# Hybrid decoder trunk on one core: the first input also as channel-major blocks, the last residual in halves

## The chip, the cores and the metric

The kernel runs on one core of a Trainium2 chip. The metric is the device time of one execution in microseconds. Before the change three runs took 2188.25, 2188.32 and 2190.48 us; their median is 2188.32 us.

The engines are named as the profile names them: PE does matrix products (PEld is its weight load), DVE is the vector engine, ACT the scalar engine, POOL the general one, SP only issues transfers. A transfer is a DMA.

## The reference, cut to what matters

```python
def rms_norm(x, g):
    y = xf * lax.rsqrt(jnp.mean(xf * xf, axis=-1, keepdims=True) + EPS)
    return y * g
...
for i in range(DEPTH):                      # two layers, 256 tokens, 2048 channels
    if i % 2 == 0:
        h = h + even_mixer(rms_norm(h, even_norm[j]), ...)   # attention | gated delta rule
    else:
        h = h + odd_mixer(rms_norm(h, odd_norm[j]), ...)     # gated position mixing
    h = h + swiglu(rms_norm(h, ffn_norm[i]), ...)
return rms_norm(h, final_norm)
```

Everything is float32. The change touches the first norm, the one ahead of `even_mixer`, and the last one.

## The kernel before

The 256 tokens are two blocks of 128 (`NT`), the 2048 channels four blocks of 512 (`NCH`), each of four blocks of 128 (`KB`). `self.h[t][n]` holds the residual stream, tokens on the partitions, 512 channels in a row.

**Products.** A product needs the channels of its input on the partitions. `fill_unit` transposes a block of `h` on PE (`tok_major`, four transposes into a `side` tile in PSUM), multiplies it by the norm's gain on DVE, and `split` makes a rounded high part on ACT and the remainder on DVE. `dense` does the same to the weights: a DMA brings a block of 512 rows into one of three `raw` buffers, ACT makes `whi`, DVE makes `wlo` (six buffers each), and PE adds three products for each token block: `whi`, `wlo` and `whi` again with the input's remainder. A block of weights is 24 such matmuls, 272 columns wide in the first projection (`kvg`: keys, values and gates of `even_mixer`), 512 wide in the others.

**Norms.** The factor 1/rms is put on after the product. `chunk_stats` squares `h` on ACT and sums along the row (`accum_out`), `end_norm` adds the four sums on DVE and takes the power on POOL; the results `rstd` are used where the sums of a product are read from PSUM.

**Order.** Every instruction is recorded in `Engine.record` (so nearly all have line 178) and `Schedule.plan` (line 189) sets each engine's order: it walks through a model of the engines, takes the ready instruction of the lowest `prio`, and lets none start ahead of its `early` time. Each engine then runs its list strictly in order. SP issues nearly all DMAs, also in order: a block of weights waits on SP until its `raw` buffer is free, and all that stands behind it on SP waits too.

**Start.** `run` (line 1026) loads the identity and the gains, then for each of four channel blocks two blocks of `h`, with the weights of `kvg` between them (`dense(first=True)`, its prio at line 483). PE transposes each block ahead of the products that use it.

**End.** `project` (line 508) writes the last 512 columns (`n = 3`), with PE's products of the second token block kept ten steps behind those of the first (`LAG`). Then `residual` adds the product to `h` on DVE, `chunk_stats` squares on ACT, DVE multiplies `h` by the final gain, and `finish` (line 1014) takes the norm and scales and stores eight blocks.

Of the kernel before, what the change touches and what calls it, by code (L numbers as in the profile page):

```python
# [10 lines left out]
F32R = mybir.dt.float32r  # L11
# [5 lines left out]
P = 128  # L17
D = 2048
# [296 lines left out]
class Trunk:  # L315
# [67 lines left out]

    def load_consts(self):
        nc, t = self.nc, self.t
        self.ident = self.keep((P, P), "ident")
        nc.sync.dma_start(self.ident, t["ident"])
        self.gains = self.const(t["gains"], [P, 4, 16], "gains")
        self.junk = self.keep((P, CW), "junk", BF16)
        self.mhalf = self.keep((P, 8), "mhalf")  # L390
        nc.vector.memset(self.mhalf, -0.5)
        self.phalf = self.keep((P, 8), "phalf")
        nc.vector.memset(self.phalf, 0.5)

    def load_tables(self):
        nc, t = self.nc, self.t
# [54 lines left out]
    def fill_unit(self, srcs, gain=None):  # L451
# [10 lines left out]
            self.split(ps, unit[t])  # L462
        return unit


    def dense(self, w, units, off, width=CW, pcs=None, lag=0, first=False):

        nc = self.nc  # L470
        ps = [self.bank(width) for _ in range(NT)]
        pcs = range(len(units)) if pcs is None else pcs
        size = P * KB * width
        todo = deque()

        def product(t, x, k, hi, lo, st, sp):
            xh, xl = x[t]
            nc.tensor.matmul(ps[t], xh[:, k], hi, start=st, stop=False)
            nc.tensor.matmul(ps[t], xh[:, k], lo, start=False, stop=False)
            nc.tensor.matmul(ps[t], xl[:, k], hi, start=False, stop=sp)  # L480

        for unit, pc in zip(units, pcs):
            with self.prio(2 * pc - 19 if first else 0):
                raw = self.slot((P, KB, width), F32, "raw")
                o = off + pc * size
                nc.sync.dma_start(raw, w[o:o + size].rearrange("(p k n) -> p k n", p=P, k=KB))
            for k in range(KB):
                with self.prio(0):
                    tags = ("unit", "unit") if lag and k % 2 else ("whi", "wlo")
                    hi, lo = [self.slot((P, width), F32R, tag) for tag in tags]  # L490
                    nc.scalar.copy(hi, raw[:, k])
                    nc.vector.tensor_tensor(lo, raw[:, k], hi.bitcast(F32), ALU.subtract)
                with self.prio(9):
                    todo.append((unit, k, hi, lo, pc == pcs[0] and k == 0, pc == pcs[-1] and k == KB - 1))
                    product(0, *todo[-1])
                    if len(todo) > lag:
                        product(1, *todo.popleft())
        with self.prio(9):
            for x in todo:
                product(1, *x)  # L500
        return ps
# [6 lines left out]
    def project(self, w, units, gain, pcs=None):  # L508

        self.begin_norm()  # L510
        size = D * CW if pcs is not None else len(units) * KB * P * CW
        for n in range(NCH):
            self.residual(n, self.dense(w, units, n * size, pcs=pcs, lag=LAG if gain is None and n == NCH - 1 else 0))
            with self.prio(1):
                if gain is not None:
                    self.units.append(self.fill_unit([self.h[t][n] for t in range(NT)], gain[:, KB * n:KB * (n + 1)]))
                self.chunk_stats(n)
                if gain is None:
                    for t in range(NT):
                        self.nc.vector.tensor_tensor(self.h[t][n], self.h[t][n], self.gf[n], ALU.mult)  # L520


    def gate_columns(self, ps):
# [354 lines left out]
    def even_mixer(self, gain):  # L878
        units = self.units
        off, mix, outs, c = 0, [], [], {}  # L880
        for name, cols in EVEN_CHUNKS:
            ps = self.dense(self.t["even_in"], units, off, chunk_width(cols), first=name == "kvg")
            off += D * chunk_width(cols)
            with self.prio(1):
                if name == "kvg":
                    self.end_norm()
                    ba, kk = self.gate_columns(ps), self.attn_kv(ps)
                else:
                    c[name] = self.zgate(ps) if name[0] == "z" else self.tok_tile(ps)
            if name == "kvg":  # L890
                self.schedule.early = 9000.0
                with self.prio(0):
                    self.load_tables()
                self.schedule.early = 0.0
                with self.prio(2):
                    self.gates(ba)
                    kT = self.attn_keys(kk)
            kind, i = name[:-1], int(name[-1]) if name[-1].isdigit() else 0
            with self.prio(2):
                if kind == "k":  # L900
                    keys = self.delta_k(i, c[name])
                elif kind == "q":
                    queries = self.delta_q(i, c[name])
                elif kind == "v":
                    outs.append(self.delta(i, keys, *queries, c[name]))
            with self.prio(3):
                if kind == "qa":
                    mix.append(self.new_unit())
                    for t in range(NT):
                        self.attention(i, t, c[name], mix[i][t], kT)  # L910
        w = self.t["even_out"]
        for n in range(NCH):
            self.residual(n, self.dense(w, mix, n * D * CW, pcs=range(0, 2)))
        with self.prio(1):
            rest = [self.delta_out(outs[i], c[f"z{i}"]) for i in range(2)]
        self.project(w, rest, gain, pcs=range(2, 4))
# [96 lines left out]

    def finish(self):
        nc = self.nc
        self.end_norm()
        for t in range(NT):
            for n in range(NCH):
                o = self.unit(shape=(P, CW))
# [6 lines left out]
    def run(self):  # L1026
        g = lambda i: self.gains[:, i]
        with self.prio(-20):
            self.load_consts()
        self.begin_norm()  # L1030
        self.h = [[None] * NCH for _ in range(NT)]
        for n in range(NCH):
            with self.prio(2 * n - 20):
                self.load_hidden(n)
            with self.prio(1):
                self.units.append(self.fill_unit([self.h[t][n] for t in range(NT)], g(0)[:, KB * n:KB * (n + 1)]))
        with self.prio(1):
            for n in range(NCH):
                self.chunk_stats(n)
        self.even_mixer(g(1))  # L1040
        self.ffn(0, g(2))
        self.odd_mixer(g(3))
        self.ffn(1, None)
        with self.prio(1):
            self.finish()
# [45 lines left out]
def arrays_of(inputs):  # L1091
# [4 lines left out]
    ctab, ident, ltri = const_table()  # L1096
    a = {
        "x": i["x"].reshape(NT, P, NCH, CW).transpose(0, 2, 1, 3),
        "ctab": ctab,
        "ident": ident,  # L1100
        "ltri": ltri,
# [41 lines left out]
```

## Time and profile before

| | |
|---|---|
| median of three runs | 2188.32 us |
| the profiled execution, own time | 2188.75 us |
| its span in the trace | 2186.7 us |
| PE busy, of the span | 2166.3 us (99%) |
| DVE busy | 1326.0 us (61%) |
| ACT busy | 1138.5 us (52%) |
| granted clock of PE, mean | 0.999 |

How to read it: PE is busy nearly all the time, so a change is worth what it takes from PE's queue or from PE's waits, at the place where these lie. The shares of DVE and ACT are means: they are higher in the first 60 us than later. A row of the timeline merges equal instructions that follow each other (x4) and gives the time from the first one's start to the last one's end; durations of neighbours overlap, so the distance between starts says what one costs in a row.

### The profile page before, as it was taken

Reading aid. Unit: us, or ns where it says so; the run is one execution under the profiler, and the core shown is the slowest. Engines: PE = TensorE matmul, PEld = TensorE weight load, DVE = VectorE, ACT = ScalarE, POOL = GpSimd, SP = SyncE. Lnnn points to the kernel's source line nnn. Section 1 sums busy time; section 2 is a strip of 40 time slices with the busy share of each in tenths; the row PEclk is TensorE's granted clock in tenths of the full one; section 3 lists DMA queues with packets and bytes.
Section 4 is the critical chain, followed back from the end, with each engine's and each line's share of the span. In section 5 each row is a group of like instructions: output and inputs, shape, how many; then the busy total and the mean of one; then the engine's idle time right before and its main releaser. Section 6 shows DMA issues by size and latency. Waiting matters only on the chain.

```text
span 2186.7 us, 27199 instructions
## 1 busy us (share of the span) xinstructions
PE 2166.3 (99%) x10044; PEld 1792.4 (82%) x10044; DVE 1326.0 (61%) x2265; ACT 1138.5 (52%) x2034; POOL 59.0 (3%) x68
## 2 busy tenths in 40 slices
PE   8999999999999999999999999999999999999998
PEld 7787888888888888888888888888888888888886
DVE  8796886765555555555555576665555555555553
ACT  7665654554545554444445545554555445444453
POOL 1010100000000000000010000000000000000000
PEclk9999999999999999999999999999999999999999
DMA  7342435555555555555565555555555555565553
GB/s 250 123 156 76 154 117 172 182 186 191 192 193 193 184 187 189 192 193 193 192 237 186 196 168 186 178 189 192 193 185 187 189 192 191 192 209 194 194 195 132
DMA packets 58453, 399.07 MB, mean 183 GB/s; under 512 B 6976, under 2 KB 7232, under 8 KB 11216
## 3 DMA queue, kind: packets, MB, share of 16 engines
q1 hardware_dynamic: 57168, 393.61, 53.0%
q0 software_dynamic: 1152, 3.74, 0.5%
q8 instruction: 78, 1.28, 0.2%
q14 instruction: 55, 0.45, 0.1%
HBM read 395.22 MB, written 2.10 MB: 182 GB/s over the span
## 4 chain that ended last, share of the span: by engine, by line
PE 96%; DVE 2%; ACT 1%; issue 1%; DMA 0%; POOL 0%; SPq 0%; POOLq 0%; DVEq 0%; ACTq 0%
PE mm L178 90%; PE side L178 6%; DVE unit L178 1%; DVE wlo L178 1%; ACT whi L178 0%; DMA h<-in_x 0%; ACT junk L178 0%; POOL unit L178 0%; DVE uc L178 0%; SPq L178 0%; DVE yt L178 0%; DVE h L178 0%; DVE yr L178 0%; ACT L178 0%; ACT unit L178 0%
## 5 line engine op out<-in xcount | busy, mean ns | idle before, releaser
L178 PE MATMUL mm<-whi,unit 128*128 128x512 f32 (+1 forms) x5864 | 1829.8, 391 | 0.0
L178 DVE TENSOR_TENSOR wlo<-raw,whi 128x512 fp32r<-128x512 f32 (+1 forms) x1466 | 1011.0, 691 | 806.0 <-ACT whi L178 800.7
L178 ACT CAST whi<-raw 128x512 fp32r<-128x512 f32 (+1 forms) x1466 | 909.1, 621 | 938.6 <-DVE wlo L178 752.6
L178 PEld LDWEIGHTS mm<-whi,unit 128*128 128x128 f32 x5864 | 1097.8, 188 | 226.0 <-issue 4.7
L178 PE MATMUL mm<-wlo,unit 128*128 128x512 f32 (+1 forms) x2932 | 1140.9, 390 | 0.0
L178 PEld LDWEIGHTS mm<-wlo,unit 128*128 128x128 f32 x2932 | 551.1, 188 | 110.8 <-issue 0.2
L178 PE MATMUL side<-unit,unit 128*128 128x128 f32 (+3 forms) x448 | 60.6, 285 | 0.0
L178 PEld LDWEIGHTS side<-unit,unit 128*128 128x128 f32 (+2 forms) x448 | 54.4, 182 | 5.6 <-issue 1.4
L178 ACT ACTIVATE unit<-mm,rstd 128x512 f32<-128x512 f32 (+1 forms) x84 | 56.1, 671 | 2.2
L178 PE MATMUL side<-ident,unit 128*128 128x128 f32 x356 | 55.0, 273 | 0.4 <-DVE unit L178 0.4
L178 PEld LDWEIGHTS side<-ident,unit 128*128 128x128 f32 x356 | 44.1, 140 | 12.2 <-issue 2.3
L178 DVE TENSOR_TENSOR unit<-side,unit 128x512 fp32r<-128x512 f32 (+1 forms) x64 | 43.6, 690 | 10.8 <-ACT unit L178 10.2
L178 ACT CAST unit<-side 128x512 fp32r<-128x512 f32 x60 | 35.1, 586 | 19.5 <-PE side L178 17.5
L178 DVE TENSOR_TENSOR unit<-unit,unit 128x512 fp32r<-128x512 f32 (+1 forms) x56 | 39.7, 714 | 1.0
L178 PE MATMUL mm<-unit,unit 128*128 128x512 f32 x132 | 35.9, 389 | 0.0
L178 ACT COPY unit<-side 128x512 f32<-128x512 f32 (+1 forms) x36 | 20.6, 585 | 25.4 <-PE side L178 25.4
L178 DVE SCALAR_TENSOR_TENSOR unit<-side,conv,unit 128x255 f32<-128x255 f32 (+2 forms) x72 | 31.1, 473 | 2.4 <-ACT unit L178 2.4
L178 ACT ACTIVATE junk<-h 128x512 bf16<-128x512 f32 x40 | 25.1, 628 | 11.1 <-DVE h L178 8.4
L178 DVE SCALAR_TENSOR_TENSOR unit<-mm,rstd,unit 128x512 f32<-128x512 f32 x44 | 30.9, 743 | 0.0
L178 DVE TENSOR_TENSOR h<-mm,h 128x512 f32<-128x512 f32 x40 | 25.8, 683 | 6.3 <-PE mm L178 6.3
L178 PEld LDWEIGHTS mm<-unit,unit 128*128 128x128 f32 x132 | 24.8, 188 | 5.1
L178 PE MATMUL side<-ident,h 128*128 128x128 f32 x128 | 20.7, 291 | 7.3 <-DMA h<-in_x 7.3
(119 smaller groups left out, 461.4 us busy)
## 6 DMA issues: line engine op xcount, KB each, us to landing
raw<-in_gate SPq DMA_DIRECT2D x88, 1024.0 KB, 4.8
raw<-in_up SPq DMA_DIRECT2D x88, 1024.0 KB, 4.8
raw<-in_down SPq DMA_DIRECT2D x88, 1024.0 KB, 4.9
raw<-in_even_in SPq DMA_DIRECT2D x40, 1024.0 KB, 4.9
raw<-in_odd_in SPq DMA_DIRECT2D x32, 1024.0 KB, 4.9
raw<-in_even_out SPq DMA_DIRECT2D x16, 1024.0 KB, 4.8
raw<-in_odd_out SPq DMA_DIRECT2D x16, 1024.0 KB, 4.9
raw<-in_even_in SPq DMA_DIRECT2D x4, 544.0 KB, 6.7
```

Of the source, the lines that this page charges most:

```text
L178: f(*map(real, args), **{k: real(a) for k, a in kw.items()})
```

## The change

- The host also lays the input out as `xt`: channels on the partitions, 4 x 128 tokens in a row, 256 KB a block as before. `first_unit` loads these eight blocks first, multiplies by the gain and splits; the first four transposes of each of the eight blocks are gone from PE.
- The first norm's sums come from the same blocks: ACT squares each, DVE adds the squares of the four channel blocks (three additions for each token block), and `first_stats` lets PE sum over the partitions, four matmuls against a column of ones for each token block.
- `h` itself is still needed for the residual; its eight DMAs are recorded with `early` 60000.
- The gains are loaded from ACT's queue, the identity later; `kvg`'s weights get another prio; the tables' `early` goes from 9000 to 12000.
- The last 512 columns: `last_chunk` adds the residual in halves of 256, squares each half on ACT as it comes, sums the first three blocks' squares ahead of the end, and multiplies by the final gain into another tile.

```diff
     def load_consts(self):
         nc, t = self.nc, self.t
-        self.ident = self.keep((P, P), "ident")
-        nc.sync.dma_start(self.ident, t["ident"])
-        self.gains = self.const(t["gains"], [P, 4, 16], "gains")
+        self.gains = self.keep((P, 4, 16), "gains")
+        nc.scalar.dma_start(self.gains, t["gains"])
+        with self.prio(-13):
+            self.ident = self.const(t["ident"], [P, P], "ident")
...
+    def first_unit(self, n, gain):
+        unit = []
+        for t in range(NT):
+            x = self.unit()
+            with self.prio(4 * n + 2 * t - 30):
+                self.nc.sync.dma_start(x, self.t["xt"][t, n])
+            with self.prio(4):
+                sq = self.unit()
+                self.nc.scalar.activation(sq, x, AF.Square)
+                if n:
+                    self.nc.vector.tensor_tensor(sq, sq, self.sq[t], ALU.add)
+                self.sq[t] = sq
+            with self.prio(1):
+                y, x = x, self.unit()
+                self.nc.vector.tensor_tensor(x, y, gain.unsqueeze(2).to_broadcast([P, KB, P]), ALU.mult)
+                unit.append([self.unit(F32R), self.unit(F32R)])
+                self.split(x, unit[t])
+        return unit
+
+    def first_stats(self):
+        self.rstd = []
+        with self.prio(4):
+            for t in range(NT):
+                tot = self.side(P, 1)
+                for k in range(KB):
+                    self.nc.tensor.matmul(tot, self.sq[t][:, k], self.ones, start=(k == 0), stop=(k == KB - 1))
+                self.rstd.append(self.rsqrt(tot, [P, 1], 1.0 / D, EPS, "rstd"))
...
-            with self.prio(2 * pc - 19 if first else 0):
+            with self.prio(4 * pc - 29 if first else 0):
...
+            if gain is None and n == NCH - 1:
+                self.last_chunk(n, self.dense(w, units, n * size, pcs=pcs, lag=LAG))
+                break
...
+    def last_chunk(self, n, ps):
+        nc = self.nc
+        half = CW // 2
+        self.rstd = []
+        with self.prio(1):
+            for t in range(NT):
+                a = self.small([P, 1], "a")
+                nc.vector.tensor_reduce(a, self.ss[t][:, :n], AX.X, ALU.add)
+                nc.vector.tensor_scalar(a, a, 1.0 / D, EPS, ALU.mult, ALU.add)
+                h, o = self.h[t][n], self.unit(shape=(P, CW))
+                cs = [slice(i * half, (i + 1) * half) for i in range(2)]
+                sq = self.small([P, 2], "sq")
+                for i, c in enumerate(cs):
+                    nc.vector.tensor_tensor(h[:, c], ps[t][:, c], h[:, c], ALU.add)
+                    nc.scalar.activation(self.junk[:, c], h[:, c], AF.Square, accum_out=sq[:, i:i + 1])
+                nc.vector.tensor_tensor(o, h, self.gf[n], ALU.mult)
+                for i in range(2):
+                    b = self.small([P, 1], "b")
+                    nc.vector.tensor_scalar(b, sq[:, i:i + 1], 1.0 / D, a, ALU.mult, ALU.add)
+                    a = b
+                r = self.small([P, 1], "rstd")
+                nc.gpsimd.tensor_tensor(r, a, self.mhalf[:, 0:1], ALU.pow)
+                self.rstd.append(r)
+                self.h[t][n] = o
...
     def run(self):
...
         for n in range(NCH):
-            with self.prio(2 * n - 20):
-                self.load_hidden(n)
-            with self.prio(1):
-                self.units.append(self.fill_unit([self.h[t][n] for t in range(NT)], g(0)[:, KB * n:KB * (n + 1)]))
+            self.units.append(self.first_unit(n, g(0)[:, KB * n:KB * (n + 1)]))
+        self.first_stats()
+        self.schedule.early = 60000.0
         with self.prio(1):
             for n in range(NCH):
-                self.chunk_stats(n)
+                self.load_hidden(n)
+        self.schedule.early = 0.0
```

What SP has to issue at the start, before. In a row stand the tile, the tensor it comes from and its size; `h` is the token-major input, `raw` the weights of `kvg`:

```order
L178 DMA ident_0_0_4484<-in_ident 128x128
L178 DMA gains_0_1_4486<-in_gains 128x64
L178 DMA h_0_4_4490<-in_x 128x512
L178 DMA h_0_5_4492<-in_x 128x512
L178 DMA raw_76_4494<-in_even_in 128x1088
L178 DMA h_0_20_4496<-in_x 128x512
L178 DMA h_0_21_4498<-in_x 128x512
L178 DMA raw_109_4500<-in_even_in 128x1088
```

And now (`unit` here holds a block of `xt`):

```order
L178 DMA unit_5_4499<-in_xt 128x512
L178 DMA raw_71_4501<-in_even_in 128x1088
L178 DMA unit_10_4505<-in_xt 128x512
L178 DMA unit_15_4509<-in_xt 128x512
L178 DMA raw_104_4511<-in_even_in 128x1088
L178 DMA unit_21_4513<-in_xt 128x512
L178 DMA unit_27_4515<-in_xt 128x512
L178 DMA raw_137_4517<-in_even_in 128x1088
```

The first weights went from the fifth place to the second, behind one block of input instead of two blocks, the identity and the gains; the second token block of the input stands behind them.

DVE's list at the start, before. `side` is the PSUM tile of the transposes, `unit_11` and `unit_18` the high parts that ACT makes:

```order
L178 TENSOR_TENSOR unit_10_4520<-side_6_4512,gains_0_1_4486 128x512
L178 TENSOR_TENSOR unit_17_4529<-side_13_4522,gains_0_1_4486 128x512
L178 TENSOR_TENSOR unit_12_4535<-unit_10_4520,unit_11_4531 128x512
L178 TENSOR_TENSOR unit_19_4539<-unit_17_4529,unit_18_4533 128x512
L178 TENSOR_TENSOR wlo_78_4550<-raw_76_4494,whi_77_4537 128x272
L178 TENSOR_TENSOR wlo_86_4557<-raw_76_4494,whi_85_4543 128x272
```

And now (`unit_5`, `unit_10` and `unit_15` are blocks of `xt`):

```order
L178 TENSOR_TENSOR unit_7_4527<-unit_5_4499,gains_0_0_4495 128x512
L178 TENSOR_TENSOR unit_9_4533<-unit_7_4527,unit_8_4531 128x512
L178 TENSOR_TENSOR unit_12_4539<-unit_10_4505,gains_0_0_4495 128x512
L178 TENSOR_TENSOR wlo_73_4543<-raw_71_4501,whi_72_4535 128x272
L178 TENSOR_TENSOR wlo_81_4549<-raw_71_4501,whi_80_4537 128x272
```

The first remainder of the weights (`wlo_73`) stands behind the multiplication of `unit_10`, the third transfer of SP's list. Further down, the additions of the squares (six of 128x512) stand between the remainders of the second projection's weights, and two rows `side<-ones,unit 128x1 x4` stand on PE among that projection's matmuls.

DVE's list at the very end, for the second token block, before; `mm` is the product, `unit_12905` the final gain:

```order
L178 TENSOR_TENSOR h_0_53_4510<-mm_14071_22892,h_0_53_4510 128x512
L178 TENSOR_TENSOR h_0_53_4510<-h_0_53_4510,unit_12905_21275 128x512
L178 TENSOR_REDUCE tot_0_14385_23276<-ss_0_13272_21890 128x1
L178 TENSOR_SCALAR rstda_0_14386_23278<-tot_0_14385_23276 128x1
L178 TENSOR_SCALAR unit_14396_23284<-h_0_5_4492,rstd_0_14387_23280 128x512
```

And now:

```order
L178 TENSOR_TENSOR h_0_70_5315<-mm_14060_22907,h_0_70_5315 128x256 x2
L178 TENSOR_TENSOR unit_14381_23296<-h_0_70_5315,unit_12894_21284 128x512
L178 TENSOR_SCALAR b_0_14382_23299<-sq_0_14378_23294,a_0_14375_22885 128x1
L178 TENSOR_SCALAR b_0_14383_23301<-sq_0_14378_23294,b_0_14382_23299 128x1
L178 TENSOR_SCALAR unit_14393_23307<-h_0_64_5298,rstd_0_14384_23303 128x512
```

The sum over the four blocks is gone from the end, the residual comes in two pieces, and the product with the gain no longer overwrites what ACT squares.

## Rows read from the trace of the kernel before

**Rows 1.** The chain of work that ended last, by engine, from the page.

```profile
PE 96%; DVE 2%; ACT 1%; issue 1%; DMA 0%; POOL 0%; SPq 0%; POOLq 0%; DVEq 0%; ACTq 0%
```

**Rows 2.** Busy time by stretch of the span: us, then busy time and instructions of PE, PEld, DVE, ACT and POOL, granted clock of PE, busy share of the DMA engines, GB/s.

```profile
4.00:10.00 6.00, 2.68 (x12) 2.31 (x13) 3.59 (x7) 4.05 (x11) 0.00 (x0) 1.00 0.99 340
24.00:50.00 26.00, 24.75 (x123) 20.45 (x122) 23.30 (x65) 17.99 (x44) 7.98 (x6) 1.00 0.56 190
120.00:180.00 60.00, 58.88 (x328) 50.04 (x327) 51.20 (x153) 35.04 (x81) 6.23 (x8) 1.00 0.41 141
240.00:300.00 60.00, 58.79 (x294) 48.54 (x293) 57.19 (x166) 37.75 (x86) 11.15 (x12) 1.00 0.46 156
600.00:2100.00 1500.00, 1500.00 (x6741) 1242.74 (x6740) 856.70 (x1276) 754.29 (x1233) 15.30 (x22) 1.00 0.56 191
```

**Rows 3.** Timeline of PE at the start: start us, us from the first start to the last end, operation, in brackets the idle time before it and what ended that.

```profile
4.58 1.94 PE L178 MATMUL side<-ident,h 128*128 128x128 f32 x8 [4.58 <-DMA h<-in_x]
9.27 1.97 PE L178 MATMUL side<-ident,h 128*128 128x128 f32 x8 [2.74 <-DMA h<-in_x]
10.88 0.80 PE L178 MATMUL mm<-whi,unit 128*128 128x272 f32 x2
11.48 0.43 PE L178 MATMUL mm<-wlo,unit 128*128 128x272 f32 x1
11.71 0.43 PE L178 MATMUL mm<-whi,unit 128*128 128x272 f32 x1
...
13.44 0.60 PE L178 MATMUL side<-ident,h 128*128 128x128 f32 x4
13.79 0.37 PE L178 MATMUL mm<-whi,unit 128*128 128x272 f32 x1
...
18.47 0.41 PE L178 MATMUL mm<-whi,unit 128*128 128x272 f32 x2
18.72 0.29 PE L178 MATMUL mm<-wlo,unit 128*128 128x272 f32 x1
...
25.91 0.75 PE L178 MATMUL mm<-whi,unit 128*128 128x272 f32 x3
26.50 0.39 PE L178 MATMUL mm<-wlo,unit 128*128 128x512 f32 x1
```

**Rows 4.** The queue of SP at the start, from its timeline.

```profile
0.74 0.39 SPq L178 DMA_DIRECT2D ident<-in_ident  x1
1.66 0.90 SPq L178 DMA_DIRECT2D h<-in_x  x2
2.60 0.43 SPq L178 DMA_DIRECT2D raw<-in_even_in  x1
```

**Rows 5.** DVE and ACT at the start, from their timelines.

```profile
4.47 0.63 ACT L178 ACTIVATE junk<-h 128x512 bf16<-128x512 f32 x1 [2.45 <-DMA h<-in_x]
8.63 1.38 ACT L178 CAST whi<-raw 128x272 fp32r<-128x272 f32 x4 [0.72 <-DMA raw<-in_even_in]
...
5.71 0.69 DVE L178 TENSOR_TENSOR unit<-side,gains 128x512 f32<-128x512 f32 x1 [4.80 <-PE side L178]
17.02 0.78 DVE L178 TENSOR_TENSOR wlo<-raw,whi 128x272 fp32r<-128x272 f32 x2
17.72 1.29 DVE L178 TENSOR_TENSOR unit<-unit,unit 128x512 fp32r<-128x512 f32 x2
23.57 0.69 DVE L178 TENSOR_TENSOR unit<-unit,unit 128x512 fp32r<-128x512 f32 x1
```

**Rows 6.** PE between 34 and 40 us, and DVE beside it, from the timeline.

```profile
34.28 0.96 PE L178 MATMUL side<-gg,unit 128*128 128x16 f32 x8
35.09 0.49 PE L178 MATMUL mm<-wlo,unit 128*128 128x512 f32 x1
...
37.37 1.54 DVE L178 TENSOR_TENSOR wlo<-raw,whi 128x512 fp32r<-128x512 f32 x1
...
40.04 0.70 PE L178 MATMUL side<-unit,one 128*128 128x512 f32 x2 [1.25 <-DVE unit L178]
```

**Rows 7.** The end, from the timeline: the last product, then what stands between it and the stores.

```profile
2176.93 0.84 PE L178 MATMUL mm<-unit,unit 128*128 128x512 f32 x3
2177.81 0.69 DVE L178 TENSOR_TENSOR h<-mm,h 128x512 f32<-128x512 f32 x1 [3.09 <-PE mm L178]
2178.59 0.63 ACT L178 ACTIVATE junk<-h 128x512 bf16<-128x512 f32 x1 [4.43 <-DVE h L178]
2179.13 0.19 ACT L178 ACTIVATION_READ_ACCUMULATOR junk<-h 128x1 f32 x1
2179.35 0.69 DVE L178 TENSOR_TENSOR h<-h,unit 128x512 f32<-128x512 f32 x1 [0.85 <-ACT junk L178]
2179.96 0.15 DVE L178 TENSOR_REDUCE tot<-ss 128x1 f32<-128x4 f32 x1
2180.14 0.15 DVE L178 TENSOR_SCALAR rstda<-tot 128x1 f32<-128x1 f32 x1
2180.37 0.55 POOL L178 TENSOR_TENSOR rstd<-rstda,mhalf 128x1 f32<-128x1 f32 x1 [6.97 <-DVE rstda L178]
```

**Rows 8.** DMA issues: KB each, median us from issue to landing; and what SP's queue waited for (us in total, times, longest).

```profile
raw<-in_even_in SPq DMA_DIRECT2D x40, 1024.0 KB, 4.9
...
SPq L178 <- DVE wlo L178: 1885.6, 355, 15.6
```

More of the change, by code (lines that the diff above doesn't have):

```diff
@@ L393, in load_consts @@
         nc.vector.memset(self.phalf, 0.5)
+        self.ones = self.keep((P, 1), "ones")
+        nc.vector.memset(self.ones, 1.0)
     def load_tables(self):
@@ L512, in project @@
         for n in range(NCH):
-            self.residual(n, self.dense(w, units, n * size, pcs=pcs, lag=LAG if gain is None and n == NCH - 1 else 0))
+            if gain is None and n == NCH - 1:
+                self.last_chunk(n, self.dense(w, units, n * size, pcs=pcs, lag=LAG))
+                break
+            self.residual(n, self.dense(w, units, n * size, pcs=pcs))
             with self.prio(1):
@@ L885, in even_mixer @@
                 if name == "kvg":
-                    self.end_norm()
                     ba, kk = self.gate_columns(ps), self.attn_kv(ps)
@@ L890, in even_mixer @@
             if name == "kvg":
-                self.schedule.early = 9000.0
+                self.schedule.early = 12000.0
                 with self.prio(0):
@@ L1015, in finish @@
         nc = self.nc
-        self.end_norm()
         for t in range(NT):
@@ L1029, in run @@
             self.load_consts()
-        self.begin_norm()
+        self.units, self.sq = [], [None] * NT
         self.h = [[None] * NCH for _ in range(NT)]
         for n in range(NCH):
-            with self.prio(2 * n - 20):
-                self.load_hidden(n)
-            with self.prio(1):
-                self.units.append(self.fill_unit([self.h[t][n] for t in range(NT)], g(0)[:, KB * n:KB * (n + 1)]))
+            self.units.append(self.first_unit(n, g(0)[:, KB * n:KB * (n + 1)]))
+        self.first_stats()
+        self.schedule.early = 60000.0
         with self.prio(1):
             for n in range(NCH):
-                self.chunk_stats(n)
+                self.load_hidden(n)
+        self.schedule.early = 0.0
         self.even_mixer(g(1))
@@ L1098, in arrays_of @@
         "x": i["x"].reshape(NT, P, NCH, CW).transpose(0, 2, 1, 3),
+        "xt": i["x"].reshape(NT, P, NCH, KB, P).transpose(0, 2, 4, 3, 1),
         "ctab": ctab,
```

## The prediction

> **What bounds the kernel now.** I read the chain of waits first: 96% of it lies on PE [rows 1]. The table by stretch says where PE is not already saturated: between 600 and 2100 us it is busy 1500.00 of 1500 us, so nothing that this change does elsewhere can help or hurt there unless it adds work to PE [rows 2]. What is left is the start, the waits of the first layer's mixer (1.1 us between 120 and 180 us, 1.2 us between 240 and 300 us, and one of 1.25 us at 38.8 us [rows 2, 6]), and the end after the last product.
>
> The start: PE waits 4.58 us for the first block of `h`, transposes, and waits 2.74 us for the next block [rows 3]. From 9.27 us on it hardly pauses; the first `kvg` matmuls show at 10.88 us, the last one starts at 25.91 us; the two behind it in that row are 512 wide and belong to the next projection [rows 3]. Beside it DVE makes all remainders, and its last one for `kvg` starts at 23.57 us [rows 5]: DVE and PE end this stage within 2 us of each other (24.26 and 26.04 us), so taking work from PE alone is not enough. At the end, 2.56 us lie between the start of the last residual (2177.81) and that of POOL's power (2180.37) [rows 7], and the stores behind it don't change.
>
> The sum is made against the profiled execution: its span is 2186.7 us, its own time 2188.75 us, and that is 0.43 us above the median of 2188.32.
>
> **The start.** I compare one point of the program: all 96 `kvg` matmuls and the next projection's first four done, since PE's new order puts those four ahead of `kvg`'s last ten. Before, `kvg` ends at about 25.91 + 0.13 = 26.04 us; four 512-wide matmuls at 0.225 us each (three take 0.84 us, one 0.39 us, so 0.45 us for two more [rows 7]) make it 26.94 us.
>
> Now the blocks of the input come in the layout that the products need, so DVE begins with the block itself: no transposes, no wait for PE. What DVE waits for is the input. Its third instruction multiplies the second token block, which is SP's third transfer, and all remainders of the weights stand behind that. When does it land? The first of the bulk transfers is issued at 0.74 us now, where the identity was, not at 1.66 us [rows 4]. Ahead of the block's end lie 256 + 32 + 544 + 256 KB = 1.11 MB; at the 340 GB/s of this stretch [rows 2] that is 3.3 us. On top comes a lag between issue and flow. Before, the first block of `h` landed at 4.47 us [rows 5], 2.8 us after its issue, of which 0.8 us are its own bytes: lag 2.0 us. The first weights landed at 8.63 us [rows 5] with 1.08 MB, 3.2 us, from the same issue: lag 3.8 us. So the block lands between 0.74 + 3.3 + 2.0 = 6.0 and 7.8 us. I take 7.0 us: the row of the first weights is the nearer one in bytes, but there the identity and the gains stood ahead, some 0.9 us of issue.
>
> From 7.0 us DVE has in its list, until the last remainder for `kvg`: 14 multiplications and remainders of the input at 0.60 us (two take 1.29 us, one 0.69 us), 8.4 us; 16 remainders of the weights at 0.35 us (two take 0.78 us, one 0.43 us), 5.5 us; two 512-wide remainders of the next projection, 1.2 us [rows 5]. That is 15.1 us, and I add 0.5 us for moments in which it waits for ACT's rounded part, so 22.6 us. Ten matmuls of 0.125 us (two starts 0.25 us apart for a pair, at 18.47 and 18.72 us [rows 3]) stand behind it: 23.9 us. PE alone would be done earlier: from about 8 us, 96 x 0.125 = 12 us, 1.8 us for a slow beginning as before (matmuls 0.23 us apart between 11.48 and 11.71 us [rows 3]) and 0.9 us, so 22.7 us; DVE decides. Gain: 26.94 - 23.9 = **3.0 us**; with the block at 7.8 us it is 2.2 us, with 6.0 us at most 4.0 us, since the second weights then decide. The 16 transposes that PE did at full pace (0.35 to 0.44 us for four, 13.44 to 13.79 us and the longer distance behind [rows 3]) and eight of the slow ones are contained in this.
>
> The rule on PE's clock in the Trainium skill (page "TensorE: Matmul & The Clock Gate", section on the HAM clock gate) speaks against thinning out PE's start: the clock is halved until the array has been kept busy, and gaps keep it halved. The granted clock reads 1.00 between 4 and 10 us, the level of 2.4 GHz [rows 2], yet matmuls lie 0.23 us apart at 11.5 us and 0.125 us at 18.5 us [rows 3], after eight transposes that were followed by a gap, so the distances agree with the rule and the column doesn't show it. By the rule the whole of `kvg` at the lower level is a rival, below; by the rows alone the slow part is the 1.8 us above.
>
> **The sums of the first norm.** Four matmuls against a column of ones, twice. The nearest row is `side<-gg,unit`, four matmuls of the program that the trace shows as eight: from 34.28 us to the next start at 35.09 us, 0.81 us [rows 6]. Twice that is **1.6 us** on PE, now bound there; if PE happens to wait for DVE, it costs 0. I take 1.6 us, because the remainders are ahead at that place. ACT's squares were there before. DVE gets six additions of 0.60 us = 3.6 us, spread between remainders. Between 24 and 50 us DVE idles 26 - 23.3 = 2.7 us [rows 2], and it reaches that stretch some 1.7 us earlier: 4.4 us of cover, so I cost it at 0; without cover it is up to 3.6 us. The sums come later by some remainders, so `kvg` is read from PSUM later; the bank is needed only after the whole next projection, 96 x 0.225 = 21.6 us, hidden. POOL's two powers and the gates behind them move along with it, and the wait of 1.25 us at 38.8 us, where DVE's remainder took 1.54 us beside POOL [rows 6], moves too: 0, with 1.25 us either way.
>
> **The later loads of `h`.** Eight issues of 0.47 us [rows 4] now stand on SP between two blocks of weights, about 60 us in. Blocks wait on SP anyway for DVE to free the buffer (1885.6 us in 355 waits [rows 8]). PE eats one block of 24 matmuls in 5.4 us, so 3.8 us of issues fit into one wait. Of 2.1 + 1.05 MB at 340 GB/s, 9.3 us, 3.9 us are left when the next block is issued; it lands 3.9 + 4.9 us [rows 8] later, 8.8 us, and is due two blocks later, at 10.8 us. Hidden, 2 us to spare. The gains on ACT's queue stand ahead of a table load with nothing behind them: 0.
>
> **The end.** First half of the residual 0.43 us (as a 272-wide remainder [rows 5]), 0.09 us to ACT, two half squares with their sums. A 512-wide square takes 0.54 us and its sum 0.19 us [rows 7]; four 272-wide casts take 1.38 us [rows 5], 0.33 us for one behind another, so a half is 0.52 us: 1.04 us. The product with the gain runs beside this. Then one small instruction of 0.15 us and 0.23 us from its start to POOL's [rows 7], which contains it, and 0.03 us ahead: 1.82 us against 2.56 us. **0.7 us** gained, between 0.3 and 0.9 us.
>
> **Sum.** 3.0 - 1.6 + 0.7 = 2.1 us. 2188.75 - 2.1 = 2186.65 us for the profiled execution, and with the 0.43 us to the median 2186.2 us. A measurement of this kernel tells some 0.2% (4.4 us) from no change, so I expect a gain that is hardly to be told.
>
> **The rivals.**
> - The lead is lost in the mixer. DVE is busy 57.19 of 60 us between 240 and 300 us and 23.30 of 26 us between 24 and 50 us [rows 2]; where PE waits for it, arriving earlier only lengthens the wait. For it: the waits of 1.1 and 1.2 us there. Against it: they are small beside the stretches, and PE does other products meanwhile. Only the end's 0.7 us stays: 2187.6 us.
> - All falls well: the block lands at 6.0 us (4.0 us), the eight small matmuls fall into waits (0), the 1.25 us wait goes: 4.0 + 0.7 + 1.25 = 5.9 us, 2182.4 us.
> - Slower, DVE: the six additions delay the remainders of the second projection. With no cover, 3.6 us of additions and 1.6 us of small matmuls stand against 3.0 + 0.7 us: 2189.8 us. It decides from the point where DVE's idle time between 24 and 50 us falls below 1.5 us.
> - Slower, PE's clock: all 96 matmuls 0.227 us apart. From 8 us that ends at 29.8 us, 30.7 us with the next four, 3.8 us after the old point, and 1.6 - 0.7 us more: 2193.0 us. Against it: at that pace PE would have no gaps, and in rows 3 unbroken work from 9.27 us brought the short distances before 13.44 us.
> - It doesn't do what it says, the late loads of `h` not hidden: they cost up to 9.3 us less the 2 us to spare, less the 2.1 us gained: 2193.5 us.
>
> **How the numbers follow.** Forecast 0.56, lead lost 0.20, all well 0.10, DVE 0.09, clock 0.03, late loads 0.02. The forecast's own bounds are: start 2.2 to 4.0, small matmuls 0 to 1.6, the wait at 38.8 us 1.25 either way, the end 0.3 to 0.9 us; together rarely beyond 2183.4 us below. Above, the range takes in the lost lead whole and most of the DVE case: to 2189.2 us. Faster by over 0.2% (below 2183.9 us): most of "all well" and a little of the forecast, 0.11. Slower by over 0.2% (above 2192.7 us): clock and late loads, 0.05. The rest, 0.84, is within.
>
> **What would show it.** In the changed profile: DVE's first multiplication ahead of 4 us, its third instruction at about 7 us, the last remainder for `kvg` ending at about 22.6 us, PE's last 272-wide matmul at about 23.9 us. Rows `side<-ones` of about 0.8 us for each group. No longer waits of PE for `wlo` between 24 and 60 us than before; raw blocks still landing in time around 60 us. At the end, 1.8 us between the first half residual and POOL's power. It is wrong if DVE's third instruction starts past 8 us, if matmuls stay 0.23 us apart past 15 us, if PE waits for remainders among the additions of squares, or if the waits between 60 and 345 us grow by what the start gained.

## The result and the profile after

The changed kernel takes 2197.35 us, median of six runs (2194.71 to 2199.18), beside 2188.86 us (2188.25 to 2190.48) for the kernel before: ratio 1.0039, 95% interval 1.0028 to 1.0049. It is 8.5 us slower, where a gain of 2.1 us was forecast (2186.2 us, with bounds of 2183.4 and 2189.2 us). The profiled execution has a span of 2195.5 us, against 2186.7 us.

First the table by stretch, with the columns of [rows 2]; the five stretches of [rows 2] are in it, and four more from 60 to 75 us.

```profile
4.00:10.00 6.00, 3.23 (x12) 2.92 (x13) 5.03 (x11) 5.33 (x12) 0.00 (x0) 1.00 1.01 387
24.00:50.00 26.00, 25.12 (x126) 20.68 (x125) 21.74 (x52) 15.57 (x35) 5.56 (x6) 1.00 0.56 198
...
60.00:63.00 3.00, 0.00 (x0) 0.00 (x0) 1.47 (x6) 1.31 (x5) 0.00 (x0) 1.00 1.00 378
...
64.00:65.00 1.00, 1.00 (x10) 0.78 (x6) 1.00 (x3) 0.00 (x0) 0.00 (x0) 0.64 1.05 402
65.00:74.00 9.00, 9.00 (x25) 6.87 (x25) 5.04 (x13) 2.91 (x10) 0.00 (x0) 0.50 0.07 26
74.00:75.00 1.00, 1.00 (x5) 0.82 (x4) 0.64 (x2) 1.00 (x5) 0.00 (x0) 0.74 0.07 16
...
120.00:180.00 60.00, 57.02 (x320) 47.60 (x318) 50.20 (x154) 35.79 (x83) 9.17 (x10) 1.00 0.38 126
240.00:300.00 60.00, 58.77 (x292) 48.78 (x291) 56.66 (x160) 37.45 (x81) 11.16 (x12) 1.00 0.44 144
600.00:2100.00 1500.00, 1500.00 (x6741) 1243.12 (x6740) 857.14 (x1276) 755.56 (x1235) 14.90 (x22) 1.00 0.57 191
```

The granted clock is the share of the full clock that PE was given. PE is idle from 60 to 63 us. It then has work without a break, and about a microsecond into that work its clock halves: granted 0.64, then 0.50 (the level of 1.2 GHz) for nine microseconds, then 0.74. In clock alone that is 0.36 + 4.5 + 0.26 = 5.1 us lost. A second loss lies between 120 and 180 us, 3.0 us idle against 1.1 us [rows 2]. In the other stretches of the table PE's idle time is as before or less.

Next the timeline of the start, PE then DVE, which answers to [rows 3, 5].

```profile
6.01 0.60 PE L178 MATMUL mm<-whi,unit 128*128 128x272 f32 x1 [6.01 <-ACT whi L178]
7.37 0.60 PE L178 MATMUL mm<-wlo,unit 128*128 128x272 f32 x1 [0.77 <-DVE wlo L178]
...
24.31 0.29 PE L178 MATMUL mm<-whi,unit 128*128 128x272 f32 x1
24.44 0.40 PE L178 MATMUL mm<-wlo,unit 128*128 128x512 f32 x1
...
28.08 0.94 PE L178 MATMUL side<-ones,unit 128*128 128x1 f32 x8
28.89 0.72 PE L178 MATMUL mm<-whi,unit 128*128 128x512 f32 x2
...
32.21 0.95 PE L178 MATMUL side<-ones,unit 128*128 128x1 f32 x8
33.02 0.49 PE L178 MATMUL mm<-wlo,unit 128*128 128x512 f32 x1
...
4.29 0.69 DVE L178 TENSOR_TENSOR unit<-unit,gains 128x512 f32<-128x512 f32 x1 [3.36 <-DMA gains<-in_gains]
...
6.28 0.69 DVE L178 TENSOR_TENSOR unit<-unit,gains 128x512 f32<-128x512 f32 x1
...
22.09 0.69 DVE L178 TENSOR_TENSOR unit<-unit,unit 128x512 fp32r<-128x512 f32 x1
```

The last `kvg` matmul gives way to the next instruction at 24.44 us. At that point the same 96 and four matmuls are done for which the prediction worked out 26.94 us before, so the start is 2.50 us shorter. Each group against the ones stands 0.81 us ahead of the next start. Now where the statistics (the sums and powers of the first norm) lead to: POOL's powers, the gates' matmuls, and what I call the decay chain, the instructions that turn the gates into the decay factors of the gated delta rule. At its end DVE and ACT read one `side` tile.

```profile
33.00 1.07 POOL L178 TENSOR_TENSOR rstd<-rstda,mhalf 128x1 f32<-128x1 f32 x2 [32.55 <-DVE rstda L178]
...
41.60 0.96 PE L178 MATMUL side<-gg,unit 128*128 128x16 f32 x8
...
46.31 0.73 PE L178 MATMUL side<-unit,one 128*128 128x512 f32 x2 [0.88 <-DVE unit L178]
...
57.73 2.26 PE L178 MATMUL side<-unit,unit 64*128 64x128 f32 x24
...
59.97 0.28 DVE L178 SCALAR_TENSOR_TENSOR unit<-side,tb,unit 128x64 f32<-128x64 f32 x1 [0.38 <-ACT unit L178]
...
60.28 0.31 ACT L178 ACTIVATE unit<-side,tail 128x64 f32<-128x64 f32 x1 [0.35 <-DVE unit L178]
...
60.63 0.28 DVE L178 SCALAR_TENSOR_TENSOR unit<-side,gam,unit 128x64 f32<-128x64 f32 x1 [0.38 <-ACT unit L178]
...
62.63 0.28 DVE L178 SCALAR_TENSOR_TENSOR unit<-side,tb,unit 128x64 f32<-128x64 f32 x1 [0.38 <-ACT unit L178]
...
63.06 1.99 PE L178 MATMUL side<-unit,unit 64*128 64x128 f32 x16 [3.07 <-DVE unit L178]
64.98 0.79 PE L178 MATMUL mm<-wlo,unit 128*128 128x512 f32 x1
```

The same places in the timeline of the kernel before:

```profile
23.50 3.43 POOL L178 TENSOR_TENSOR rstd<-rstda,mhalf 128x1 f32<-128x1 f32 x2 [23.05 <-DVE rstda L178]
...
53.87 0.27 DVE L178 SCALAR_TENSOR_TENSOR unit<-side,tb,unit 128x64 f32<-128x64 f32 x1
...
54.80 0.71 ACT L178 ACTIVATE unit<-side,tail 128x64 f32<-128x64 f32 x3
...
57.76 4.60 PE L178 MATMUL side<-unit,unit 64*128 64x128 f32 x48
```

The powers are done some 7 us later (34.07 against 26.93 us). The gates' matmuls stand at 41.60 us against 34.28 us [rows 6]. The first attention's score matmuls begin at the same time in both, 57.7 us. Before, DVE's last read of the last decay tile had ended at 54.1 us and ACT's at 55.5 us, and the score matmuls ran through. Now the last read ends at 62.9 us, 7.4 us later. On the way DVE waits 0.38 us for ACT and ACT waits 0.35 us for DVE, with a read of DVE every 0.67 us. There are four `side` tiles, three groups of scores fill three by 59.99 us (57.73 + 2.26), and the fourth belongs to the chain until its last read; 0.15 us after that PE goes on.

The second loss is one wait for POOL:

```profile
122.87 0.50 PE L178 MATMUL side<-unit,same 128*128 128x512 f32 x1 [2.19 <-POOL unit L178]
```

Last the end, which answers to [rows 7]. From the first half residual to POOL's power it is 2.01 us, where it was 2.56 us.

```profile
2187.23 0.76 DVE L178 TENSOR_TENSOR h<-mm,h 128x256 f32<-128x256 f32 x2 [3.59 <-PE mm L178]
2187.75 0.42 ACT L178 ACTIVATE junk<-h 128x256 bf16<-128x256 f32 x1 [4.66 <-DVE h L178]
...
2188.94 0.21 DVE L178 TENSOR_SCALAR b<-sq,b 128x1 f32<-128x1 f32 x1
2189.24 0.55 POOL L178 TENSOR_TENSOR rstd<-b,mhalf 128x1 f32<-128x1 f32 x1 [6.91 <-DVE b L178]
```

### The profile page after: what moved, and what is told of

The parts are those of the page before. It is cut to its first block, busy times and chain, and to the rows that moved or that the text cites. A ratio compares the mean times of both kernels' runs of the same rounds, so it can differ in the third digit from the quotient of the medians.

```text
span 2195.5 us, 27173 instructions
## 1 busy us (share of the span) xinstructions
PE 2171.2 (99%) x10028; PEld 1794.0 (82%) x10028; DVE 1329.6 (61%) x2276; ACT 1139.0 (52%) x2030; POOL 57.5 (3%) x68
## 4 chain that ended last, share of the span: by engine, by line
PE 95%; DVE 3%; ACT 1%; issue 1%; POOL 0%; DMA 0%; POOLq 0%; DVEq 0%; ACTq 0%
PE mm L178 89%; PE side L178 6%; DVE unit L178 1%; DVE wlo L178 1%; ACT whi L178 0%; POOL unit L178 0%; ACT unit L178 0%; DMA gains<-in_gains 0%; DVE uc L178 0%; ACT junk L178 0%; DVE yt L178 0%; DVE yr L178 0%; ACT L178 0%; POOLq L1199 0%; DVE ucp L178 0%
## 5 line engine op out<-in xcount | busy, mean ns | idle before, releaser
L178 DVE SCALAR_TENSOR_TENSOR unit<-side,conv,unit 128x254 f32<-128x254 f32 (+2 forms) x72 | 30.5, 474 | 3.9 <-ACT unit L178 3.7
L178 DVE TENSOR_TENSOR h<-mm,h 128x512 f32<-128x512 f32 (+1 forms) x42 | 26.0, 658 | 6.8 <-PE mm L178 6.8
L178 ACT ACTIVATE junk<-h 128x512 bf16<-128x512 f32 (+1 forms) x34 | 20.5, 602 | 8.5 <-DVE h L178 8.4
L178 ACT CAST unit<-unit 128x512 fp32r<-128x512 f32 x32 | 19.8, 618 | 9.6 <-DVE unit L178 9.4
```

The costliest lines, as they stand in the source:

```text
L178: f(*map(real, args), **{k: real(a) for k, a in kw.items()})
```

## The experiments

Theory A: late statistics push the decay chain into the first attention; PE waits 3.1 us, and its clock then halves. Rival B: the eight late loads of `h`, which run from 56 to 65 us with the DMA engines full, do it. Rival C: it is the wait of 2.2 us for POOL near 122 us, and the other order of instructions up to 165 us. The first three kernels set these against each other. Each ratio below is to the kernel before, timed beside that run.

**Statistics early again (e1)**, in `first_unit` and `first_stats`:

```
-            with self.prio(4):
+            with self.prio(1):
```

> The changed kernel with one number altered: the first norm's squares, additions and ones matmuls get priority 1 in the planner in place of 4, so that the statistics, and with them the gates and the decay chain, come as early as they did before the change. Theory A (late statistics push the decay chain into the first attention's score matmuls, TensorE idles 3.1 us and its granted clock then falls to 0.5 for some 10 us): both are gone, what is left is the start's 2.5 us less the 1.6 us of the ones matmuls and the 0.55 us of the end, 2188.9 - 1.5 = 2187.4 us, 2185.5 to 2189.0. Rival B (the eight late loads of h saturate the DMA engines at 56 to 65 us and hold the weights up): they are as late as in the changed kernel, so the stall stays, about 2197 us. Rival C (the waits of 2.2 us on GpSimd near 122 us and the other order up to 165 us cost most of it): most of the 8.5 us stays, above 2192 us.

Measured: 2188.54 us, ratio 1.0002 (0.9992 to 1.0011). The loss of 8.5 us is gone, and so are the wait at 60 us and the wait for POOL. That speaks against B, but doesn't settle it: the loads of `h` kept their `early` time, and yet SP issues them at 64.15 us here, against 56.45 us in the changed kernel. 2188.5 us is a microsecond above A's 2187.4 us, inside A's range. The squares and additions now stand among the casts and remainders at the start, and PE waits there for DVE and ACT. Its timeline, in the profile of the one run of ten that took 2193.7 us (the other nine lie between 2188.2 and 2189.7 us):

```profile
8.49 0.59 PE L178 MATMUL mm<-wlo,unit 128*128 128x272 f32 x1 [2.39 <-DVE wlo L178]
...
15.93 0.39 PE L178 MATMUL mm<-whi,unit 128*128 128x272 f32 x1 [1.37 <-ACT unit L178]
...
20.59 1.70 PE L178 MATMUL side<-ones,unit 128*128 128x1 f32 x8
...
44.27 0.73 PE L178 MATMUL side<-unit,one 128*128 128x512 f32 x2 [1.82 <-DVE unit L178]
```

What sets this run apart is a granted clock of 0.50 in two places, from 19 to 25 us behind the wait of 1.37 us (and one of 0.69 us at 17.13 us), and from 46 to 49 us behind the wait of 1.82 us. So in this profile early statistics cost PE waits at the start, where the changed kernel has 0.77 and 0.64 us of them. That the microsecond in the medians comes from these waits isn't shown; the interval is wider than a microsecond.

**Loads of `h` later (e2)**, in `run`:

```
-        self.schedule.early = 60000.0
+        self.schedule.early = 150000.0
```

> The changed kernel with the eight loads of h given to the queue 13 blocks of weights later (planner time 150 us in place of 60 us); the order on TensorE, VectorE, ScalarE and GpSimd is untouched, word for word. Theory A: the stall at 60 us and the half clock behind it stay, 2197.4 us, 2195.5 to 2199. Rival B: without the loads at 56 to 65 us the stall is gone, about 2187.4 us. Rival C: 2197.

Measured: 2197.77 us (2193.73 to 2198.16), ratio 1.0034 (1.0020 to 1.0048), as A said. The wait of 3.07 us is there again (at 62.65 us). The DMA engines have nothing to do behind it, and PE is at half its clock all the same; in a row stand PE's busy time and instructions, the granted clock, the DMA share and GB/s:

```profile
65.00:70.00 5.00, 5.00 (x17) 0.50 0.00 0
```

B is out.

**The kernel before with late sums (e3)**, in `even_mixer`:

```
+                    self.schedule.early = 28000.0
                     self.end_norm()
+                    self.schedule.early = 0.0
```

> The kernel before the change with one alteration: the two reductions and powers of the first norm may not be planned before 28 us of the planner's time, so that the gates come some 5 to 8 us later than they did, as in the changed kernel; loads, squares, transposes of the start and the end stay as before. Theory A: the decay chain now meets the first attention, TensorE waits 2 to 4 us near 60 us and its granted clock falls, 2188.9 + 3 to 9 = 2192 to 2198 us. Rivals B and C (late loads of h, or the changed start): neither is in this kernel, 2188.9 us, 2188 to 2190.

Measured: 2191.04 us, ratio 1.0011 (1.0002 to 1.0021); nine runs at 2190.0 to 2192.2 us and one at 2195.7 us, with a mean granted clock of 0.996 where the nine have 0.999. Late sums alone, with the old start, loads and end, cost 2.2 us. That is under A's 3 to 9 us and above what B and C allow (2188 to 2190 us). The powers come as late as in the changed kernel (they end at 33.63 us), and the timeline of the first run (2192.24 us) shows the collision, smaller:

```profile
57.28 2.26 PE L178 MATMUL side<-unit,unit 64*128 64x128 f32 x24
60.66 1.71 PE L178 MATMUL side<-unit,unit 64*128 64x128 f32 x16 [1.12 <-ACT unit L178]
```

Here the two engines read the tile in longer pieces, DVE seven times in a row 0.19 us apart. That suggests that the lateness needs a second thing to make PE wait 3 us, the turns; e5 tests it. The wait accounts for 1.12 of the 2.2 us; where the rest lies isn't shown.

**The end alone (e4)**, `last_chunk` and `finish` of the changed kernel in the kernel before (the diff is the change's own).

> The kernel before the change with the last chunk alone done by halves. By the traces the last matmul to the last power is 0.55 us shorter in the changed kernel, so 2188.9 - 0.55 = 2188.3 us under every theory of the middle; a rival in which the shorter end is lost to the last stores gives 2188.9.

Measured: 2188.14 us, ratio 0.9995 (0.9986 to 1.0004). The 0.7 us agree with the trace, and the interval doesn't tell them from nothing.

**DVE's reads of the last decay tile in one piece (e5)**, after the plan:

```
+        h = self.tiles[self.whole]
+        reads = [op for op in order if op.engine == "dve" and h in op.tiles]
+        i = order.index(reads[0])
+        rest = [op for op in order if op not in reads]
+        order = rest[:i] + reads + rest[i:]
...
+            if gr == 1 and t == 1:
+                self.schedule.whole = rep.tensor.name
```

(`rep` is the decay tile; the one marked is the last of the four.)

> The changed kernel; the order on TensorE, ScalarE, GpSimd and the queues is untouched, and on VectorE the eight reads of the last decay tile in PSUM stand in one piece, ahead of one weight remainder, where that remainder had stood behind the first of them; the eight reads of the same tile by ScalarE then stand behind all of VectorE's, where they had stood between them in turn. Theory A, refined: the two engines' reads of one PSUM tile wait for each other in the written order, which in the changed kernel makes eight steps of 0.67 us (57.84 to 62.9 us) and holds the tile that the fourth group of score matmuls needs until 63.06; in one piece the eight take 1.6 us on VectorE and about 1 us more on ScalarE, the tile is free near 60.5 us, the wait falls from 3.07 to 0.3 to 1.0 us and the half clock behind it goes: 2197.4 - 2.4 - 5.1 = 2189.9 us, 2188.5 to 2192. If the clock falls for another reason than the wait: 2195. If the wait is the sum of the engines' work and not their turns: 2197.

Measured: 2191.16 us, ratio 1.0018 (1.0008 to 1.0027). Seven of ten runs lie at 2190.6 to 2192.2 us (mean granted clock 0.998 to 0.999), three at 2194.9 to 2195.8 us (0.996 to 0.997). Timelines of DVE, ACT and PE in the profile of one of the three:

```profile
58.92 0.28 DVE L183 SCALAR_TENSOR_TENSOR unit<-side,gam,unit 128x64 f32<-128x64 f32 x1
59.12 0.27 DVE L183 SCALAR_TENSOR_TENSOR unit<-side,tb,unit 128x64 f32<-128x64 f32 x1
...
60.15 1.33 ACT L183 ACTIVATE unit<-side,tail 128x64 f32<-128x64 f32 x6
...
61.54 1.71 PE L183 MATMUL side<-unit,unit 64*128 64x128 f32 x16 [1.62 <-ACT unit L183]
```

and two stretches of its table, with the columns as for e2, the second with the wait ahead of it:

```profile
65.00:70.00 5.00, 5.00 (x16) 0.50 0.09 31
...
119.82 0.50 PE L183 MATMUL side<-unit,same 128*128 128x512 f32 x1 [2.19 <-POOL unit L183]
121.00:125.00 4.00, 4.00 (x13) 0.57 0.46 195
```

One remainder on DVE changed its place, and nothing else. DVE's reads come 0.19 us apart, not 0.67, and PE's wait falls from 3.07 to 1.62 us (expected 0.3 to 1.0). ACT needs 2.1 us behind DVE's last read, where about 1 us had been expected: six of its reads take 1.33 us, and one more and a 512-wide instruction stand ahead of them. The turns were 1.45 us of the wait. The lower mean clock comes in three runs of ten, not in all. In the profiled one of the three, PE drops to half its clock twice, behind the wait of 1.62 us and behind the wait of 2.19 us for POOL; which of the two it was in the other runs isn't shown. The seven other runs have a median of 2190.97 us.

**The first attention behind the chain (e6)**, in `even_mixer`, the statistics as late as before:

```
+                    self.schedule.early = 62000.0
                     for t in range(NT):
                         self.attention(i, t, c[name], mix[i][t], kT)
+                    self.schedule.early = 0.0
```

> The changed kernel with the first attention not planned before 62 us of the planner's time, so that its score matmuls stand behind the decay chain and projection matmuls fill TensorE meanwhile; the statistics stay as late as in the changed kernel. Theory A: no wait near 60 us, the granted clock stays at 1.00, 2189.5 us, 2187.5 to 2191. If late statistics cost by themselves, through the gates or the projections that need the powers: the loss stays, above 2194.

Measured: 2186.80 us, ratio 0.9993 (0.9983 to 1.0002). The whole loss is gone, and the time lies below A's 2189.5 us and its range: the wait for POOL near 122 us, which A's figure had kept, is gone as well. The powers come as late as in the changed kernel (33.31 us against 33.00 us), so late statistics don't cost by themselves.

**The kernel before, made to wait (e7, e8)**, in the first attention:

```
+            if kv == 0 and t == 0 and r == 0:
+                self.schedule.unseen = True
+                for i in range(8):
+                    nc.vector.tensor_tensor(s[:, :, 0], qT, qT, ALU.add)
+                self.schedule.unseen = False
```

(While `unseen` is set, the planner counts an instruction at 0 us; e8 has `range(4)`.)

> The kernel before the change with eight additions of 0.60 us (128x512, results overwritten) ahead of the first attention's first mask addition on VectorE, counted at nothing by the planner, so that every other instruction stands where it stood. By the rows of before the first mask addition moves from 59.2 to 64.0 us, and TensorE, which has three groups of scores and one free PSUM tile ahead of it, waits about 3 us. Theory A (a wait of 3 us at this place is followed by some 10 us at half clock): 2188.8 + 3 + 5 = 2196.8 us, 2194 to 2198, granted clock 0.50 behind the wait. If the clock of the changed kernel fell for another reason (its start, its loads, its other order): 2188.8 + 3 = 2191.8 us and a granted clock of 1.00.

> The same with four additions: the first mask addition moves by 2.4 us, and TensorE waits about 0.6 us. Theory A: a short wait leaves the clock at 1.00, 2188.8 + 0.6 = 2189.4 us, 2188.5 to 2190.5. If any wait here makes the clock fall: 2194.

Measured with eight additions: 2195.27 us, ratio 1.0033 (1.0019 to 1.0046), mean granted clock 0.997 in all five runs (0.998 to 0.999 in the 26 of the kernel before). With four: 2189.38 us, ratio 1.0004 (0.9995 to 1.0014), 0.998 to 0.999 in all ten, behind a wait of 0.36 us. PE's timeline with eight:

```profile
57.06 3.16 PE L179 MATMUL side<-unit,unit 64*128 64x128 f32 x32
63.36 3.21 PE L179 MATMUL side<-unit,unit 64*128 64x128 f32 x16 [3.14 <-DVE unit L179]
66.50 0.79 PE L179 MATMUL mm<-whi,unit 128*128 128x512 f32 x1
```

and one stretch of its table, with the columns as for e2:

```profile
65.00:70.00 5.00, 5.00 (x16) 0.50 0.01 3
```

Nothing of the change is in this kernel: old start, old loads, old statistics, old order. A wait of 3.14 us is followed by half the clock. POOL's first power of the next norm comes 6.2 us later (451.14 against 444.99 us), although this profile was 0.7 us ahead at the first powers (22.81 against 23.50 us), so the two cost about 6.8 us; the medians say 7.0 us. This shows the second half of A by itself.

**The better kernel once more, and its control (e9, e10).** The control is the same delay of the first attention in the kernel before.

> The kernel of e6_attention_later again, word for word, timed in more rounds, since its interval touched no change: with the wait and the half clock gone, what the change gains at its start (2.5 us) and end (0.55 us) less the ones matmuls (1.62 us) should be left, 1.4 us below the kernel before, about 2187 us, ratio 0.9993 (0.9988 to 0.9998). If the gain of 1.5 us was chance: ratio 1.000.

> The kernel before the change with the same delay of the first attention as in e6_attention_later and nothing else: in the kernel before, the first attention met no wait, so by theory A the delay brings nothing, 2188.5 us, ratio 1.000 (0.9995 to 1.0005). If the delay of the attention is a gain by itself (another order up to 170 us), this kernel falls by about 1.5 us too, ratio 0.9993, and the gain of e6_attention_later says nothing of the change's start and end.

Measured: 2186.36 us, ratio 0.9988 (0.9979 to 0.9997), and for the control 2189.78 us, ratio 1.0006 (0.9997 to 1.0015). The delay by itself brings nothing (the control's interval holds 1), so the gain is the change's own. The terms give 1.4 us, the two measurements 1.5 us (e6) and 2.4 us (e9). PE's table of the better kernel, where the changed one stood still and then ran at half pace:

```profile
60.00:65.00 5.00, 5.00 (x24) 1.00 0.50 167
65.00:74.00 9.00, 9.00 (x67) 1.00 0.75 286
```

## Why the prediction was wrong

The step that failed is in "The sums of the first norm": "POOL's two powers and the gates behind them move along with it, and the wait of 1.25 us at 38.8 us [...] moves too: 0, with 1.25 us either way." The wait did move as said (0.88 us, at 46.31 us). What was left out is who meets the gates when they come 7 us later. I followed the sums to the one reader whose deadline I knew, the `kvg` bank, and found it hidden. I didn't follow the gates to the end of their chain, the decay tiles, and didn't set that end, 55.5 us, beside the time at which PE wants the fourth `side` tile for the scores, 60.0 us (57.76 us and three groups, 2.26 us). There were 4.5 us of room, and the end moved by 7.4 us: 2.9 us too many, and 0.15 us until PE goes on make the wait of 3.07 us. Nor did the prediction count what follows such a wait on PE, the half clock.

Its list of signs did hold the place: "if the waits between 60 and 345 us grow by what the start gained". They grew by more. The rival "the lead is lost in the mixer" (0.20, 2187.6 us) named the place too, but by another mechanism (an early arrival that only lengthens a wait) and at no more than the lead.

The sum by terms, against what ran:
- The start: 3.0 us said, 2.50 us measured (24.44 against 26.94 us). DVE's first instruction came at 4.29 us, not ahead of 4 us: it waited for the gains, which the prediction had at 0. Its third came at 6.28 us, said 7.0; the last remainder ended at 22.78 us, said 22.6. "DVE decides" didn't come true: from 20.37 us on PE ran to 24.44 us without a wait, so its own queue set the end. The half microsecond that is missing has the size of PE's wait of 0.64 us for ACT at 20.37 us, which the sum didn't hold.
- The ones matmuls: 1.6 us said, 2 x 0.81 us measured.
- The additions: 0 said. Late, they made no remainder late: PE has no wait for `wlo` behind 7.37 us. Early, the statistics have a time one to two microseconds longer (e1: 2188.5 us, where e6 and e9 have 2186.8 and 2186.4 us), which the intervals don't separate. That rival's mechanism (additions ahead of remainders) didn't happen in the changed kernel, though its sign did.
- The late loads: hidden said, and nothing contradicts it: without them at that place (e2) the time is the same.
- The end: 0.7 us said, 0.55 us in the trace; e4's median is 0.7 us lower, with an interval that holds 0.
- The sum: said 2186.2 us. With the collision taken out, and all else of the change kept, it is 2186.8 and 2186.4 us (e6, e9). The terms that were in it were sized well; what was missing is five times as large as their sum.

What is missing, in numbers: POOL's first power of the next norm starts at 454.43 us in the changed kernel and at 443.61 us in the profile of e9, 10.8 us apart, of which 0.45 us stands already at the first powers (33.00 against 32.55 us). The wait is 3.07 us, the half clock 5.1 us, the wait for POOL near 122 us 2.19 us, together 10.4 us. The first two are shown by e5, e6 and e7. The third, `side<-unit,same` at 122.87 us, is absent in e1, e6 and e9, but no kernel took it away alone, so its price is only read off the row. One comparison agrees with it: e5 keeps this wait and one of 1.62 us, e6 has neither, and the seven runs of e5 without the lower clock are 4.2 us above e6. What brings it is open. Late gates alone don't: e3 has them and lacks this wait.

The rival on PE's clock, 2193.0 us with a chance of 0.03, named the right thing in the wrong place. It put the half clock at the start, 3.8 us of it; at the start the pace hardly changed (matmuls are 0.125 us apart from 13.43 us on, before from 13.19 us on), and the half clock came in the mixer, 5.1 us behind a wait that no rival had. The Trainium skill (page "TensorE: Matmul & The Clock Gate", section "HAM oscillation — how this bites in real kernels") says that a wait for a DMA between stretches of matmuls can put the array back to half its clock, so that the next stretch starts slow. The trace agrees, for a wait of another kind (for a free PSUM tile): 0.50 from 65 to 74 us, behind 3.07 us without a matmul.

## What to carry to other kernels

When a change delays a small result, follow it through every engine to the last instruction that depends on it, and set that time beside the next work that wants the same engine or the same buffers; a deadline met at the first reader says little. Price a wait on a saturated TensorE (PE) at what follows it as well: here 3.07 us of idleness cost 8.2 us. And where a planner sets the order, a delay can be given back at its collision: moving the one consumer (the first attention) turned 8.5 us of loss into a gain of 1.5 us (e6) or 2.4 us (e9).

## What the hardware showed that I had not expected

- One wait in an otherwise full TensorE can bring the half clock, and it then stays for long although the engine has work without a break: 10 us in the changed kernel, nearly 7 us in the profiles of e5 and e7, and about 13 us in e2.
- The length of the wait alone doesn't tell whether it comes. In the profiles it came behind 3.07 us (the changed kernel, e2) and 3.14 us (e7), and behind 1.37 us (with 0.69 us shortly after) and 1.82 us (both e1) and 1.62 us (e5). It did not come behind 1.25 us (before, at 40.04 us), 1.12 us (e3) and 0.36 us (e8). One and the same wait, 2.19 us for POOL near 120 us, was followed by it in the profile of e5 and not in those of the changed kernel and of e2, where the granted clock stays at 1.00. Of the other runs only the mean clock is known: with the waits of over 3 us it is 0.995 to 0.997 in 15 of 16 runs and 0.998 in one of e2 (2193.73 us); it is low in three of ten runs of e5 and in one of ten of e3 and e1 each.
- Where DVE and ACT read one PSUM tile in turns, a read of each took 0.67 us together, while DVE's reads in a row come 0.19 us apart. Each change of engine shows as a wait in the trace (0.38 and 0.35 us). With DVE's reads written in one piece (e5) ACT waits once, 1.69 us.
